# Strassen's seven products in ten of the 32 units of a state-space output projection, and block sums formed in place

## The chip, the core and the metric

The kernel runs on one core of one Trainium2 chip. TensorE (PE) does the matrix multiplications and accumulates in PSUM, which has eight banks of 128 x 512 floats here; ScalarE (ACT) and VectorE (DVE) do the elementwise work; SyncE's queue (SP) issues the weight loads from HBM. The metric is the device time of one execution in microseconds. Of the kernel before, three runs took 1952.21, 1953.63 and 1956.0 us: the median is 1953.63.

## What is computed

One layer of a bidirectional hybrid encoder over 256 tokens with model width 2048: latent attention and a state-space (SSD) branch side by side, gated and mixed, an output projection, then a gated feed-forward with a small convolution, and a final norm. Two places matter here:

```
y = rms_norm(y * silu(z), norm_w)                    # (256, 4096)
s = y @ w_o_ssd                                      # (256, 4096) @ (4096, 2048)
mixed = sigmoid(g_attn) * attn_out + sigmoid(g_ssd) * s
h = h + mixed @ w_out
...
h = h + (silu(gate) * val) @ w_down                  # (256, 5632) @ (5632, 2048)
out = rms_norm(h, norm_final_w)
```

All data are float32. Every product of the dense layers is made of three matrix multiplications on numbers cut into a high part (float32r, the tiles named `...h` or index 0) and the low rest: high x high, high x low and low x high.

## The kernel before

All dense layers are one list of **jobs**; a job owns one weight tile `raw` of up to 1 MB (16 blocks of 128 x 128). A `raw` is loaded by one queue (SP), three of them at a time (`RAWB=3`). It is then cut in **halves** of eight blocks: ScalarE copies a half to `wh` (the high part), VectorE subtracts it from `raw` to give `wl`. Of `wh` and of `wl` there are five buffers each (`HB=5`), so a half can be cut only when TensorE is through with the half five before it. The main loop walks the jobs in order, and before a job's matrix multiplications are issued it asks for the halves up to five ahead (`ahead`, `split_to`). Other work is hung on jobs as side functions (`at(slot, fn)`), and the framework's scheduler settles the final order on each engine; each engine then runs its own list strictly in that order.

**The SSD output projection** (`os`) takes 32 jobs made by `quad`: for each of four groups of 512 output columns, eight jobs of four K tiles. The activations `yHL` are the stationary operand (one 128 x 128 block for 128 tokens), the weights move in blocks of 512 columns; so each job is 4 K tiles x 2 token halves x 3 = 24 matrix multiplications. Each group has two PSUM banks (`g`). When a group ends, `os_evac` scales the sums by the token's norm factor, multiplies by the gate, adds the attention part (`mixS`, reloaded from HBM), and `mix_channels` transposes the result into `mHL`, which the output projection `w_out` then uses. `ssd_split` applies the norm weight and cuts `y` into `yHL` before.

**The down projection** (`w_dn`) already uses Strassen's form (Winograd's variant) in ten jobs, five in each of the first two parts of the feed-forward (`seven_jobs`): a job holds a 256 x 1024 piece of the weights as the four blocks B11, B12, B21, B22, each 128 x 512, and makes seven block products of three matrix multiplications each, 21 in place of 24. The weights' side needs four block sums; `split_seven` forms them in pages of their own, `T13` (B11+B12 and B22+B12) and `T24` (their sum with B22, and that plus B21), in four halves `h` = 0 to 3:

```
if h == 0:   cut B11, B21                      -> products of A11 and A12 use wh/wl
elif h == 1: T1 = B11+B12, T3 = B22+B12; cut T1, T3     (1024 columns)
elif h == 2: T2 = T1+B22, T4 = T2+B21;  cut B22, T2     (512 + 512)
else:        cut T4                                     (512)
```

The activations' sums (`act_sums`) are made when the activations are. In this part of the kernel the seven-product jobs (called S below) alternate with ordinary `w_dn` jobs (called P), whose stationary operand is the weight: 16 matrix multiplications of 512 columns with `wh`, then 16 of 256 columns with `wl`.

Of the kernel before, what the change touches and what calls it, by code (L numbers as in the profile page):

```python
# [47 lines left out]
class Job:  # L48


    def __init__(self, src, nb, mm, evac):
# [12 lines left out]
def tile_bidir_hybrid_layer(ctx: ExitStack, tc, xT, pos, vec, cst, w_in, w_r, w_v, w_qk, w_oa,  # L64
# [53 lines left out]
    def load(i):  # L118
# [26 lines left out]
    sums = {}  # L145

    def split_seven(i, h, wh, wl):
# [32 lines left out]
    def split_to(n):  # L180
        while hptr[0] < min(n, len(halves)):
# [823 lines left out]
    def act_sums(kp, e, o):  # L1005
        t0, t1 = slice(0, P), slice(P, S)
        w = page([P, 4, P], name="asum")
        W1, R, N4, N2 = (w[:, i, :] for i in range(4))
        dve.tensor_sub(W1, e[:, t1], o[:, t1])
        dve.tensor_sub(R, e[:, t1], e[:, t0])  # L1010
        dve.tensor_sub(N2, e[:, t0], W1)
        dve.tensor_sub(N4, o[:, t0], N2)
        t = aS[kp] = page([P, 2, 4, P], F32R, name="aS")
        act.activation(t[:, 0], w, AF.Copy)
# [501 lines left out]
```

## Time and profile before

| | |
|---|---|
| time, median of three runs | 1953.63 us (1952.21 to 1956.0) |
| span of the profiled execution | 1949.9 us |
| PE busy | 1935.2 us, 99% |
| DVE busy | 1502.5 us, 77% |
| ACT busy | 1219.2 us, 63% |

The profile shows one execution. No time of its own is given for that execution beside its span, which is 3.7 us below the median of the timed runs. In rows of the timeline a start and a duration are given in microseconds, then engine, line, operation, tiles and shapes; matrix multiplications are pipelined, so the distance from start to start, not the duration, is what one costs. "[1.12 <-DVE ...]" at a row's end is the idle time of the engine before that instruction and what ended it.

### The profile page before, as it was taken

How to read it: one execution, taken by the hardware profiler on the slowest of the kernel's cores; microseconds unless marked ns; L12 is line 12 of the kernel's file. 1: busy time of each engine (PE TensorE's matmuls, PEld its weight loads, DVE VectorE, ACT ScalarE, POOL GpSimd, SP SyncE). 2: the span in 40 equal slices, each digit the busy share in tenths (PEclk: the TensorE clock that was granted, in tenths of full speed). 3: DMA queues.
4: the chain of work that ended last, by engine and by line, in shares of the span. 5: the costliest groups of instructions: out<-in, count | busy, mean ns of one | idle time of the engine just before them, and what ended most of it. 6: DMA issues, size and time to landing. Idle time of an engine off the chain costs nothing.

```text
span 1949.9 us, 28969 instructions
## 1 busy us (share of the span) xinstructions
PE 1935.2 (99%) x10978; PEld 1695.1 (87%) x10978; DVE 1502.5 (77%) x2498; ACT 1219.2 (63%) x1930; POOL 16.2 (1%) x36
## 2 busy tenths in 40 slices
PE   9999999999999999999999999999999999999997
PEld 8899988888888888888888888888888888888887
DVE  8887765779779879879755566888887887987775
ACT  6566544687887887978644455665555655545563
POOL 0200000000000000000000000000000000000000
PEclk9999999999999999999999999999999999999999
DMA  8644456765665565565666565555556555564553
GB/s 287 200 162 152 136 176 220 248 221 171 213 237 172 198 235 187 202 216 175 207 192 204 197 215 174 194 192 183 185 179 218 186 197 192 181 208 176 204 166 125
DMA packets 103771, 379.57 MB, mean 195 GB/s; under 512 B 11216, under 2 KB 21904, under 8 KB 75472
## 3 DMA queue, kind: packets, MB, share of 16 engines
q1 hardware_dynamic: 101840, 375.09, 56.8%
q8 instruction: 86, 1.41, 0.3%
q0 software_dynamic: 1024, 1.54, 0.3%
q10 hardware_dynamic: 768, 1.09, 0.2%
q14 instruction: 53, 0.43, 0.1%
HBM read 372.08 MB, written 4.42 MB: 193 GB/s over the span
## 4 chain that ended last, share of the span: by engine, by line
PE 96%; DVE 2%; DMA 1%; ACT 1%; issue 0%; SPq 0%; DVEq 0%; ACTq 0%
PE g L224 41%; PE g L231 22%; PE g L259 7%; PE g L260 7%; PE g L261 7%; PE g L203 1%; PE g L205 1%; PE g L204 1%; PE s L853 1%; PE s L862 1%; DMA raw<-in_w_dn 1%; DVE wl L198 1%; PE s L203 0%; PE s L205 0%; PE s L204 0%; PE s L1040 0%
## 5 line engine op out<-in xcount | busy, mean ns | idle before, releaser
L198 DVE TENSOR_TENSOR wl<-raw,wh 128x1024 fp32r<-128x1024 f32 (+2 forms) x654 | 778.9, 1200 | 267.3 <-ACT wh L197 187.5
L197 ACT ACTIVATE wh<-raw 128x1024 fp32r<-128x1024 f32 (+2 forms) x654 | 676.4, 1040 | 375.9 <-PE g L261 156.8
L224 PE MATMUL g<-xHL,wh 128*128 128x512 f32 x1424 | 341.6, 392 | 0.2 <-DVE cu L284 0.2
L224 PE MATMUL g<-hHL,wh 128*128 128x512 f32 x1408 | 327.8, 390 | 0.0
L224 PEld LDWEIGHTS g<-xHL,wh 128*128 128x128 f32 x1424 | 262.5, 188 | 52.0 <-PE s L205 0.4
L224 PEld LDWEIGHTS g<-hHL,wh 128*128 128x128 f32 x1408 | 261.5, 188 | 52.4
L231 PEld LDWEIGHTS g<-xHL,wl 128*128 128x128 f32 x1424 | 182.6, 191 | 7.0
L231 PE MATMUL g<-xHL,wl 128*128 128x256 f32 x1424 | 184.7, 283 | 0.0
L231 PEld LDWEIGHTS g<-hHL,wl 128*128 128x128 f32 x1408 | 174.8, 192 | 3.4
L231 PE MATMUL g<-hHL,wl 128*128 128x256 f32 x1408 | 176.0, 283 | 0.0
L974 DVE SCALAR_TENSOR_TENSOR uc<-u,V,uc 128x255 f32<-128x255 f32 x176 | 84.3, 479 | 57.8 <-ACT uc L972 56.3
L224 PE MATMUL g<-aHL,wh 128*128 128x512 f32 x532 | 127.0, 391 | 1.1 <-DVE aHL L992 1.1
L972 ACT ACTIVATE uc<-u,V 128x256 f32<-128x256 f32 x88 | 52.3, 595 | 115.7 <-DVE u L291 115.7
L224 PEld LDWEIGHTS g<-aHL,wh 128*128 128x128 f32 x532 | 98.4, 188 | 21.7 <-DVE aHL L992 2.3
L259 PE MATMUL g<-wh,xHL 128*128 128x512 f32 x256 | 100.2, 391 | 0.0
L259 PE MATMUL g<-wh,yHL 128*128 128x512 f32 x256 | 100.1, 391 | 0.0
L260 PE MATMUL g<-wl,xHL 128*128 128x512 f32 x256 | 99.9, 390 | 0.0
L261 PE MATMUL g<-wh,yHL 128*128 128x512 f32 x256 | 99.7, 389 | 0.0
L261 PE MATMUL g<-wh,xHL 128*128 128x512 f32 x256 | 99.6, 389 | 0.0
L260 PE MATMUL g<-wl,yHL 128*128 128x512 f32 x256 | 99.6, 389 | 0.0
L231 PEld LDWEIGHTS g<-aHL,wl 128*128 128x128 f32 x532 | 67.9, 191 | 2.4
L231 PE MATMUL g<-aHL,wl 128*128 128x256 f32 x532 | 69.0, 283 | 0.0
(336 smaller groups left out, 2750.2 us busy)
## 6 DMA issues: line engine op xcount, KB each, us to landing
raw<-in_w_in SPq DMA_DIRECT2D x88, 1024.0 KB, 4.9
raw<-in_w_up SPq DMA_DIRECT2D x88, 1024.0 KB, 5.0
raw<-in_w_in SPq DMA_DIRECT2D x128, 256.0 KB, 3.9
raw<-in_w_os SPq DMA_DIRECT2D x128, 256.0 KB, 3.5
raw<-in_w_dn SPq DMA_DIRECT2D x26, 1024.0 KB, 5.1
raw<-in_w_oa SPq DMA_DIRECT2D x64, 256.0 KB, 3.9
FB<-acsD SPq DMA_DIRECT2D x32, 512.0 KB, 7.6
raw<-in_w_out SPq DMA_DIRECT2D x14, 1024.0 KB, 4.9
```

The lines of the kernel that those rows point to most:

```text
L197: act.activation(vh, r, AF.Copy)
L198: dve.tensor_sub(vl, r, f32(vh))
L203: pe.matmul(ps, lhsT=wH, rhs=xH, start=first, stop=False)
L204: pe.matmul(ps, lhsT=wH, rhs=xL, start=False, stop=False)
L205: pe.matmul(ps, lhsT=wL, rhs=xH, start=False, stop=last)
L224: pe.matmul(ps, lhsT=wh[:, b, :], rhs=x, start=k == 0, stop=False)
L231: pe.matmul(cell["ps"][:, 0, :], lhsT=wl[:, b, :], rhs=get(k)[:, 0, :], start=False, stop=k == ktot - 1)
L259: pe.matmul(ps, lhsT=x[:, 0, ts], rhs=wH[:, kk, :], start=k == 0, stop=False)
L260: pe.matmul(ps, lhsT=x[:, 0, ts], rhs=wL[:, kk, :], start=False, stop=False)
L261: pe.matmul(ps, lhsT=x[:, 1, ts], rhs=wH[:, kk, :], start=False, stop=k == kt - 1)
L972: act.activation(o, u, AF.Identity, scale=vcol("fcw", 88 + cb), bias=vcol("fcb", cb))
L974: dve.scalar_tensor_tensor(o[:, a], u[:, b], vcol("fcw", k * 88 + cb), o[:, a], ALU.mult, ALU.add)
```

## The change

- **The projection `os` is rebuilt as two runs** of 16 jobs (`os_run`), run n for output columns 1024n to 1024n+1023. A job holds one pair of K tiles (256 rows) for all eight output blocks. It is either ordinary (24 matrix multiplications) or of seven products (21); both add into the same PSUM banks, four of the pool `g` (M2, M3, M4 and P22) and four of the pool `s` (M1, M5, M6, M7). Four jobs of the first run and six of the second are of seven products; they are written S10, S11, and so on, in the strings `runs`. At the end of a run `inner` and `outer` combine the banks.
- **The block sums of the weights are formed in place** in `raw` by `split_seven`, which the down projection's ten jobs use too; the pages `T13` and `T24` are gone.
- **`ssd_split`** scales `y` in place first (four ScalarE operations of 256 columns) and then cuts it by 512 columns; `ssd_sums` makes the activations' sums for groups 3, 5 and 7 (`ySh`, `ySl`).
- **`os_evac` becomes `mix_in`**, done for a whole run: the first run's two column groups are mixed in the second run, the second run's in the first jobs of `w_out`. For that the first four output blocks of `w_out`, not two, are done in two halves of K, in banks of the pool `s`.
- A job's weights come by one load of 1 MB with pieces of 1 KB, in place of four loads of 256 KB with pieces of 2 KB.

```diff
+    def hilo(wh, wl, v):
+        act.activation(wh, v, AF.Copy)
+        dve.tensor_sub(wl, v, f32(wh))
...
         if h == 0:
-            parts(lambda w: w.rearrange("p (k m) c -> p m k c", k=2), r[:, :4])
+            vh, vl = (w.rearrange("p (k m) c -> p m k c", k=2) for w in (wh, wl))
+            hilo(vh, vl, r[:, :4])
         elif h == 1:
-            t = page([P, 2, 4, P], name="T13")
-            dve.tensor_add(t[:, 0], B11, B12)
-            dve.tensor_add(t[:, 1], B22, B12)
-            parts(both, t)
-            sums["T1"] = t[:, 0]
+            dve.tensor_add(B11, B11, B12)
+            dve.tensor_add(B12, B22, B12)
+            hilo(wh, wl, r[:, :, 0, :])
         elif h == 2:
-            t = page([P, 2, 4, P], name="T24")
-            dve.tensor_add(t[:, 0], sums.pop("T1"), B22)
-            dve.tensor_add(t[:, 1], t[:, 0], B21)
-            parts(one(0), B22)
-            parts(one(1), t[:, 0])
-            sums["T4"] = t[:, 1]
+            dve.tensor_add(B11, B11, B22)
+            hilo(wh[:, :4, :], wl[:, :4, :], B22)
+            hilo(wh[:, 4:, :], wl[:, 4:, :], B11)
         else:
-            parts(one(0), sums.pop("T4"))
+            dve.tensor_add(B21, B11, B21)
+            hilo(wh[:, :4, :], wl[:, :4, :], B21)
...
     def ssd_split(g):
+        y = ypg[g]
+        for k in range(4):
+            act.activation(y[:, k, :], y[:, k, :], AF.Identity, scale=vcol("ssdn", 4 * g + k))
         for b in range(2):
             t = page([P, 2, 2, S], F32R, name="yHL")
-            for j in range(2):
-                k = 2 * b + j
-                w = vcol("ssdn", 4 * g + k)
-                act.activation(t[:, 0, j, :], ypg[g][:, k, :], AF.Identity, scale=w)
-                dve.scalar_tensor_tensor(t[:, 1, j, :], ypg[g][:, k, :], w, f32(t[:, 0, j, :]),
-                                         ALU.mult, ALU.subtract)
+            hilo(t[:, 0], t[:, 1], y[:, 2 * b:2 * b + 2, :])
...
+    SEVEN = ((("M1", "A11"), ("M2", "A12")), (("M5", "W1"), ("M7", "R")), (("M3", "N4"), ("M6", "N2")),
+             (("M4", "A22"),))
...
+        def add(nm, aH, aL, bH, bL):
+            if nm not in M:
+                M[nm] = spsum([P, 512]) if nm in ("M1", "M5", "M6", "M7") else gpsum([P, 512])
+            for x, w in ((aH, bH), (aH, bL), (aL, bH)):
+                pe.matmul(M[nm], lhsT=x, rhs=w, start=left[nm] == total[nm], stop=left[nm] == 1)
+                left[nm] -= 1
+
+        def inner():
+            c, v = page([P, 2, 512], name="m15"), page([P, 2, 512], name="vx")
+            m1, m5, V, X = c[:, 0, :], c[:, 1, :], v[:, 0, :], v[:, 1, :]
+            act.activation(m1, M["M1"], AF.Copy)
+            act.activation(m5, M["M5"], AF.Copy)
+            dve.tensor_sub(V, M["M6"], m1)
+            dve.tensor_add(X, M["M7"], V)
+            dve.tensor_add(V, V, m5)
+            dve.tensor_add(m5, X, m5)
+            res.update({(0, 0): m1, (1, 0): X, (0, 1): V, (1, 1): m5})
+
+        def outer(h):
+            for t, nm in ((0, ("M2", "M3")[h]), (1, ("M4", "P22")[h])):
+                o = res[t, h]
+                dve.tensor_tensor(o, M[nm], o, ALU.subtract if nm == "M4" else ALU.add)
+            cap(n, h, res)
...
-    def os_evac(q, t, ps):
-        if t == 0:
-            mixT[q] = page([P, 2, 512], name="ms")
-        o = mixT[q][:, t, :]
-        act.activation(o, ps, AF.Copy, scale=r_ssd["t"][:, t:t + 1])
-        dve.scalar_tensor_tensor(o, ts_[q][:, t, :], 1.0, o, ALU.add, ALU.mult)
-        dve.tensor_add(o, o, mixS[q][:, t, :])
+    def mix_in(q, res):
+        g = mixT[q] = mixS[q]
+        for t in range(2):
+            o = res[t, q % 2]
+            dve.scalar_tensor_tensor(o, ts_[q][:, t, :], 1.0, o, ALU.add, ALU.mult)
+            dve.scalar_tensor_tensor(g[:, t, :], o, r_ssd["t"][:, t:t + 1], g[:, t, :], ALU.mult, ALU.add)
...
-    at(b + 6, ssd_r)
-    for q in range(4):
-        jobs += quad(lambda m: OsSrc(m), q, 32, lambda k: pair(yHL, k), os_evac)
-        at(len(jobs) + (1 if q < 3 else 2), mix_channels, q)
+    runs = "0 1 2 3 4 5 8 S10 9 S11 6 S14 7 S15 12 13", "0 1 2 3 4 S6 5 S7 8 S10 9 S11 12 S14 S15 13"
...
+    for g, i in ((5, 4), (7, 7), (3, 11)):
+        at(b + i, ssd_sums, g)
...
+    at(b + 17, ssd_r)
+    for q in range(2):
+        at(b + 17 + q, mix_load, q)
+        at(b + 19 + q, lambda q: mix_in(q, done[0]), q)
+        at(b + 20 + q, mix_channels, q)
+        at(b + 25 + q, mix_load, 2 + q)
```

What this makes of the instruction lists is shown at three places on VectorE. The first is the down projection, the third S job of its first part; before, `T13` and `T24` are the pages of block sums, `wl` the low halves of the weights, `h` the residual that an ordinary job adds to:

```order
L166 TENSOR_TENSOR T13_13705<-raw_13671 128x512 [waits DMAHW3_49]
L1099 TENSOR_TENSOR h_11106<-h_11106,g_13632 128x256 [waits PE_49]
L198 TENSOR_TENSOR wl_13674<-raw_13621,wh_13673 128x1024 [waits DMAHW2_49,Activation_49]
L1099 TENSOR_TENSOR h_11106<-h_11106,g_13632 128x256 [waits DVE_49]
L167 TENSOR_TENSOR T13_13705<-raw_13671 128x512
L198 TENSOR_TENSOR wl_13684<-raw_13621,wh_13683 128x1024 [waits Activation_49]
L155 TENSOR_TENSOR wl_13694<-raw_13671,wh_13693 128x4x2x128 [waits Activation_49]
L172 TENSOR_TENSOR T24_13717<-T13_13705,raw_13671 128x512
L155 TENSOR_TENSOR wl_13704<-T13_13705,wh_13703 128x1024 [waits Activation_49]
L173 TENSOR_TENSOR T24_13717<-T24_13717,raw_13671 128x512 [waits DVE_49]
L155 TENSOR_TENSOR wl_13716<-raw_13671,wh_13715 128x512 [waits Activation_49]
L155 TENSOR_TENSOR wl_13716<-T24_13717,wh_13715 128x512 [waits Activation_49]
```

The same S job after the change, where the sums overwrite `raw`:

```order
L148 TENSOR_TENSOR wl_13755<-raw_13732,wh_13754 128x4x2x128 [waits DMAHW5_49,Activation_49]
L159 TENSOR_TENSOR raw_13732<-raw_13732 128x4x128 [waits DVE_49]
L160 TENSOR_TENSOR raw_13732<-raw_13732 128x4x128 [waits DVE_49]
L148 TENSOR_TENSOR wl_13765<-raw_13732,wh_13764 128x1024 [waits Activation_49]
L148 TENSOR_TENSOR wl_13776<-raw_13732,wh_13775 128x512 [waits Activation_49]
L163 TENSOR_TENSOR raw_13732<-raw_13732 128x4x128 [waits DVE_49]
L1159 TENSOR_TENSOR h_11171<-h_11171,g_13782 128x256 [waits PE_49]
L167 TENSOR_TENSOR raw_13732<-raw_13732 128x4x128 [waits DVE_49]
L148 TENSOR_TENSOR wl_13776<-raw_13732,wh_13775 128x512 [waits Activation_49]
L1159 TENSOR_TENSOR h_11171<-h_11171,g_13782 128x256 [waits DVE_49]
L148 TENSOR_TENSOR wl_13808<-raw_13732,wh_13807 128x512 [waits Activation_49]
```

The first two sums no longer stand ahead of the first `wl` with the preceding job's cuts between them; all four stand behind it, and the second `wl` follows the second sum at once.

The second place is VectorE in the new `os` stage, the job S11 of the first run and the ordinary job behind it; before, this stage had only the cuts of ordinary halves (`L198`), two a job:

```order
L148 TENSOR_TENSOR wl_9886<-raw_9851,wh_9885 128x4x2x128 [waits DMAHW4_49,Activation_49]
L159 TENSOR_TENSOR raw_9851<-raw_9851 128x4x128 [waits DVE_49]
L160 TENSOR_TENSOR raw_9851<-raw_9851 128x4x128 [waits DVE_49]
L148 TENSOR_TENSOR wl_9897<-raw_9851,wh_9896 128x1024 [waits Activation_49]
L148 TENSOR_TENSOR wl_9908<-raw_9851,wh_9907 128x512 [waits Activation_49]
L163 TENSOR_TENSOR raw_9851<-raw_9851 128x4x128 [waits DVE_49]
L167 TENSOR_TENSOR raw_9851<-raw_9851 128x4x128 [waits DVE_49]
L148 TENSOR_TENSOR wl_9908<-raw_9851,wh_9907 128x512 [waits Activation_49]
L148 TENSOR_TENSOR wl_9927<-raw_9851,wh_9926 128x512 [waits Activation_49]
L191 TENSOR_TENSOR wl_9946<-raw_9905,wh_9945 128x4x2x128 [waits DMAHW5_49,Activation_49]
L191 TENSOR_TENSOR wl_9956<-raw_9905,wh_9955 128x4x2x128 [waits Activation_49]
```

An S job now has nine VectorE instructions in a row, an ordinary job two.

The third place is VectorE at the end of the second run, behind the job S14: the job S15 (`raw_10749`), the first operation of `inner` (`vx`, from the PSUM bank M6) and the last ordinary job, 13 (`raw_10787`):

```order
L148 TENSOR_TENSOR wl_10790<-raw_10749,wh_10789 128x4x2x128 [waits DMAHW5_49,Activation_49]
L159 TENSOR_TENSOR raw_10749<-raw_10749 128x4x128 [waits DVE_49]
L160 TENSOR_TENSOR raw_10749<-raw_10749 128x4x128 [waits DVE_49]
L148 TENSOR_TENSOR wl_10800<-raw_10749,wh_10799 128x1024 [waits PE_49,Activation_49]
L148 TENSOR_TENSOR wl_10812<-raw_10749,wh_10811 128x512 [waits PE_49,Activation_49]
L163 TENSOR_TENSOR raw_10749<-raw_10749 128x4x128 [waits DVE_49]
L167 TENSOR_TENSOR raw_10749<-raw_10749 128x4x128 [waits DVE_49]
L148 TENSOR_TENSOR wl_10812<-raw_10749,wh_10811 128x512 [waits Activation_49]
L148 TENSOR_TENSOR wl_10825<-raw_10749,wh_10824 128x512 [waits PE_49,Activation_49]
L939 TENSOR_TENSOR vx_10874<-s_10495,m15_10873 128x512 [waits PE_49]
L191 TENSOR_TENSOR wl_10835<-raw_10787,wh_10834 128x4x2x128 [waits DMAHW6_49,Activation_49]
L191 TENSOR_TENSOR wl_10845<-raw_10787,wh_10844 128x4x2x128 [waits Activation_49]
```

Here two S jobs follow one another, and `inner`'s first operation, which waits for TensorE, stands ahead of the cuts of job 13.

## Rows read from the trace of the kernel before

**Rows 1.** The page: busy time by engine (share of the span).

```profile
PE 1935.2 (99%) x10978; PEld 1695.1 (87%) x10978; DVE 1502.5 (77%) x2498; ACT 1219.2 (63%) x1930; POOL 16.2 (1%) x36
```

**Rows 2.** Waits of TensorE: total us, times, longest us.

```profile
PE g L1332 <- DVE xw L335: 1.6, 3, 1.1
PE g L224 <- DVE aHL L992: 1.1, 1, 1.1
...
PE g L224 <- DVE cu L284: 0.2, 1, 0.2
```

**Rows 3.** Windows: length, busy PE, PEld, DVE, ACT, POOL; clock; DMA share, GB/s.

```profile
935.00:1117.00 182.00, 182.00 (x851) 151.41 (x850) 105.29 (x120) 87.83 (x108) 0.00 (x0) 1.00 0.60 194
1400.00:1450.00 50.00, 50.00 (x260) 42.96 (x259) 45.40 (x62) 29.34 (x35) 0.00 (x0) 1.00 0.57 187
1940.00:1949.90 9.90, 0.71 (x4) 0.52 (x4) 5.13 (x10) 0.00 (x0) 0.00 (x0) 0.64 0.55 212
```

**Rows 4.** PE timeline in the old projection, 24 matrix multiplications apart.

```profile
950.00 0.39 PE L259 MATMUL g<-wh,yHL 128*128 128x512 f32 x1
...
955.44 0.39 PE L259 MATMUL g<-wh,yHL 128*128 128x512 f32 x1
```

**Rows 5.** PE timeline in the down projection: S, then P, then S.

```profile
1408.59 0.40 PE L1038 MATMUL s<-wh,aHL 128*128 128x512 f32 x1
...
1413.38 3.79 PE L224 MATMUL g<-aHL,wh 128*128 128x512 f32 x16
1417.01 2.08 PE L231 MATMUL g<-aHL,wl 128*128 128x256 f32 x16
1418.92 0.40 PE L1038 MATMUL s<-wh,aHL 128*128 128x512 f32 x1
```

**Rows 6.** DVE timeline in the down projection, third S job.

```profile
1404.88 0.68 DVE L173 TENSOR_TENSOR T<-T,raw 128x512 f32<-128x512 f32 x1
1405.49 0.68 DVE L155 TENSOR_TENSOR wl<-raw,wh 128x512 fp32r<-128x512 f32 x1
...
1412.68 1.23 DVE L155 TENSOR_TENSOR wl<-raw,wh 128x1024 fp32r<-128x1024 f32 x1
1413.82 0.69 DVE L172 TENSOR_TENSOR T<-T,raw 128x512 f32<-128x512 f32 x1
1414.43 1.22 DVE L155 TENSOR_TENSOR wl<-T,wh 128x1024 fp32r<-128x1024 f32 x1
...
1419.88 0.41 DVE L1099 TENSOR_TENSOR h<-h,g 128x256 f32<-128x256 f32 x1
1420.21 1.22 DVE L198 TENSOR_TENSOR wl<-raw,wh 128x1024 fp32r<-128x1024 f32 x1
```

**Rows 7.** ACT timeline in the same stretch.

```profile
1405.68 0.63 ACT L154 ACTIVATE wh<-T 128x512 fp32r<-128x512 f32 x1 [0.96 <-DVE T L173]
...
1412.95 1.06 ACT L154 ACTIVATE wh<-T 128x1024 fp32r<-128x1024 f32 x1 [0.30 <-PE g L1040]
1413.91 0.62 ACT L154 ACTIVATE wh<-raw 128x512 fp32r<-128x512 f32 x1
```

**Rows 8.** DVE timeline: a single tap, and two taps of which the second needs the first.

```profile
1380.48 1.00 DVE L974 SCALAR_TENSOR_TENSOR uc<-u,V,uc 128x255 f32<-128x255 f32 x2 [1.75 <-ACT uc L972]
...
1387.47 0.47 DVE L974 SCALAR_TENSOR_TENSOR uc<-u,V,uc 128x255 f32<-128x255 f32 x1
1387.87 0.41 DVE L284 TENSOR_TENSOR u<-u,g 128x256 f32<-128x256 f32 x1
```

**Rows 9.** PE timeline: transposes of one `mix_channels`.

```profile
1122.42 1.03 PE L926 MATMUL s<-CT,ms 128*128 128x128 f32 x8
1123.22 2.77 PE L224 MATMUL g<-mHL,wh 128*128 128x512 f32 x10
```

**Rows 10.** PE timeline at the wait for `aHL`.

```profile
1395.01 0.73 PE L224 MATMUL g<-aHL,wh 128*128 128x512 f32 x2 [1.12 <-DVE aHL L992]
```

**Rows 11.** DVE timeline at the same place.

```profile
1393.93 0.69 DVE L166 TENSOR_TENSOR T<-raw 128x512 f32<-128x512 f32 x1 [1.45 <-DMA raw<-in_w_dn]
1394.54 0.42 DVE L992 TENSOR_TENSOR aHL<-uc,aHL 128x256 fp32r<-128x256 f32 x1
```

**Rows 12.** DMA issues: KB each, us from issue to landing.

```profile
raw<-in_w_os SPq DMA_DIRECT2D x128, 256.0 KB, 3.5
raw<-in_w_dn SPq DMA_DIRECT2D x26, 1024.0 KB, 5.1
...
mixS<-mixD SPq DMA_DIRECT2D x4, 512.0 KB, 5.9
```

More of the change, by code (lines that the diff above doesn't have):

```diff
@@ L189, in split_to @@
                 continue
-            if jobs[i].quad:
+            if jobs[i].wide:
+                r = raws[i].rearrange("p (m k) c -> p m k c", m=8)[:, 4 * h:4 * h + 4]
+                vh, vl = (w.rearrange("p (k m) c -> p m k c", k=2) for w in (wh, wl))
+            elif jobs[i].quad:
                 r = raws[i].rearrange("p (m k) c -> p m k c", m=4)[:, :, 2 * h:2 * h + 2, :]
@@ L904, in ssd_split, with sums_of, ssd_sums @@
-            yHL[2 * g + b] = t
+            hilo(t[:, 0], t[:, 1], y[:, 2 * b:2 * b + 2, :])
+            yHL[2 * g + b] = t
+    def sums_of(w, e, o):
+        t0, t1 = slice(0, P), slice(P, S)
+        W1, R, N4, N2 = w
+        dve.tensor_sub(W1, e[..., t1], o[..., t1])
+        dve.tensor_sub(R, e[..., t1], e[..., t0])
+        dve.tensor_sub(N2, e[..., t0], W1)
+        dve.tensor_sub(N4, o[..., t0], N2)
+    yS = {}
+    def ssd_sums(g):
+        y = ypg[g]
+        w = page([P, 4, 2, P], name="ysum")
+        sums_of([w[:, i] for i in range(4)], y[:, 0::2, :], y[:, 1::2, :])
+        hi, lo = page([P, 4, 2, P], F32R, name="ySh"), page([P, 4, 2, P], F32R, name="ySl")
+        hilo(hi, lo, w)
+        for b in range(2):
+            yS[2 * g + b] = hi[:, :, b, :], lo[:, :, b, :]
@@ new lines, in tile_bidir_hybrid_layer, with seven_left, os_run, unit @@
+    SEVEN = ((("M1", "A11"), ("M2", "A12")), (("M5", "W1"), ("M7", "R")), (("M3", "N4"), ("M6", "N2")),
+             (("M4", "A22"),))
+    def seven_left(pr, st, nm):
+        if nm in ("A11", "A12", "A22"):
+            k, t = int(nm[2]) - 1, int(nm[1]) - 1
+            return [pr[:, i, k, t * P:(t + 1) * P] for i in range(2)]
+        i = ("W1", "R", "N4", "N2").index(nm)
+        return [a[:, i, :] for a in st]
+    def os_run(n, order, cap):
+        M, left, res = {}, {}, {}
+        for kp, sv in order:
+            for nm, c in ([(nm, 1) for hh in SEVEN for nm, _ in hh] if sv
+                          else [(nm, 2) for nm in ("M2", "M3", "M4", "P22")]):
+                left[nm] = left.get(nm, 0) + 3 * c
+        total = dict(left)
+        sevens_left = [sum(sv for _, sv in order)]
+        def add(nm, aH, aL, bH, bL):
[19 more added lines that the diff above has]
+            cap(n, h, res)
+        def unit(i, kp, sv):
+            def mm(h, nb, wh, wl):
+                if sv:
+                    for a, (nm, lf) in enumerate(SEVEN[h]):
+                        aH, aL = seven_left(yHL[kp], yS[kp], lf)
+                        add(nm, aH, aL, *(w[:, 4 * a:4 * a + 4, :].rearrange("p m c -> p (m c)")
+                                          for w in (wh, wl)))
+                else:
+                    wH, wL = (w.rearrange("p (k m) c -> p k (m c)", k=2) for w in (wh, wl))
+                    for k in range(2):
+                        for t, nm in ((0, ("M2", "M3")[h]), (1, ("M4", "P22")[h])):
+                            aH, aL = (yHL[kp][:, j, k, t * P:(t + 1) * P] for j in range(2))
+                            add(nm, aH, aL, wH[:, k, :], wL[:, k, :])
+                    if i == len(order) - 1:
+                        outer(h)
+            def ev():
+                if sv:
+                    sevens_left[0] -= 1
+                    if sevens_left[0] == 0:
+                        inner()
+            kh, kk = kp // 8, 2 * kp % 16
+            j = Job(w_os[8 * n:8 * n + 8, kh, :, kk:kk + 2, :].rearrange("m p k c -> p m (k c)"), 16, mm, ev)
+            j.wide, j.seven = True, sv
+            if sv:
+                j.nh = 4
+            return j
+        assert not order[-1][1] and not order[0][1]
+        return [unit(i, kp, sv) for i, (kp, sv) in enumerate(order)]
@@ L1005, in act_sums @@
     def act_sums(kp, e, o):
-        t0, t1 = slice(0, P), slice(P, S)
         w = page([P, 4, P], name="asum")
[L1008 to L1014, printed above, removed]
-        dve.tensor_sub(t[:, 1], w, f32(t[:, 0]))
+        sums_of([w[:, i, :] for i in range(4)], e, o)
+        t = page([P, 2, 4, P], F32R, name="aS")
+        hilo(t[:, 0], t[:, 1], w)
+        aS[kp] = t[:, 0], t[:, 1]
     def seven_jobs(p):
```

63 lines of the change are left out of this document (26 added, 37 removed).

## The prediction

> **What bounds the kernel now.** The page comes first: TensorE is busy 99% of the span, VectorE 77%, ScalarE 63% [rows 1]. The waits of TensorE come next: outside start and end only 1.1 and 0.2 us are lost [rows 2]. So the time is the sum of TensorE's work, and a change gains what it takes off TensorE, minus the waits that it makes. Whether it makes any is read by stage: in the old SSD projection TensorE is busy for 182.00 of 182 us and VectorE for 105.29; in the down projection, where products of seven already run, TensorE is busy for 50.00 of 50 and VectorE for 45.40 [rows 3]. VectorE has room in the first stage and little in the second. An average says nothing about a short chain, so the rest goes by chains. S is a job of seven products, P an ordinary one.
>
> **Off TensorE.** 24 matrix multiplications take 955.44 - 950.00 = 5.44 us, 0.227 each [rows 4]; 21 in an S take 4.79 [rows 5], the same pace. Ten S jobs save 3 each: 30 x 0.227 = 6.8 us. Transposes and the four tiny sums of squares are as many as before.
>
> **Added to VectorE and ScalarE.** On VectorE 1024 columns cost 1.14 us from start to start, 512 cost 0.61 [rows 6]. An S needs two of the first and seven of the second, 6.5 us; a P needs two of the first, 2.3. Ten S: +42 us. The sums of three activation groups (four of 256 columns at 0.33 and one of 1024 each [rows 6]) are +7.4, the two ends of runs +9.7 (16 x 0.61), and cutting y by 512 saves some 3. Together 56 us on 105, in a stage of 182 - 7 = 175: 92%, and waiting within the chains is not yet in it. ScalarE's extra copies fit: 87.83 of 182 was busy [rows 3], and about 25 come on top (1.6 us an S, 1.0 for each of eight groups of y, from the copies' pitch [rows 7]).
>
> **The chain of one S.** Before, the first two sums needed only the load and were done ahead of time; in place they must wait until both engines have read `raw`. From rows: a VectorE operation that needs the one before it starts 0.12 later than a free one (two taps take 1.00, where one takes 0.47 and lets the next start after 0.40) [rows 8]; ScalarE starts 0.12 after the sum that it waits for ended (1404.88 + 0.68 to 1405.68) [rows 6, 7]; its copy of 1024 columns takes 1.06 (0.96 to the next), of 512 0.63 (0.52 to the next) [rows 7]; I let VectorE follow 0.07 later. Counted from the start of the first `wl`:
> - first sum 1.27, second 2.00, ended 2.68; ScalarE copies 2.80 to 3.86; second `wl` 3.93. VectorE stands still for 1.3 us, since the next instruction in its list is this one.
> - `wl` of B22 5.07, third sum 5.68, fourth 6.41, ended 7.09; `wl` of T2 7.17, of T4 7.90.
> - the P behind it: copies from 7.73 and 8.70, `wl` 8.86 and 10.00; the next S at 11.14.
>
> TensorE needs 45 x 0.227 = 10.2 for the pair. So a pair is bound by VectorE and loses 0.9 us, once the cover is used up. **Cover** is the time by which an S's first `wl` is ahead of TensorE's start on that S. The five buffers limit it; before it was 1418.92 - 1412.68 = 6.2 [rows 5, 6]. Needed is: P's first `wl` complete (8.86 + 1.22 = 10.08) when TensorE reaches its 22nd matrix multiplication behind the S's start (5.0): 5.1.
> - **Run 1, pairs S10 to S15:** cover 6.2, 5.3, 4.4: the third waits 0.7, the fourth 0.9: **+1.6** (0.7 to 2.5, as the activation sums of three groups stand in the same stretch).
> - **Run 2, S6 to S11:** 1.03 us of transposes [rows 9] in front of S6 holds TensorE back and restores cover; **+1.0** (0 to 2).
> - **S14 and S15 together, then 13.** S14 has 4.2 of cover left. S15's first `wl` comes at 8.9, its fourth cut at 16.8; then `inner` waits for M6, and the first `wl` of job 13 stands behind that, complete at 19.3. TensorE wants it at 43 x 0.227 = 9.8. Needed 9.5, there 4.2: 5.3; some four products that need only `wh` stand ahead, 0.9: **+4.4** (2.5 to 6).
> - **PSUM and the hand-over to `w_out`:** M5, M7 and M6 need banks that the transposes' cuts free just in time; the second run's mixing has four first halves of `w_out`, some 11 us, as cover: **+0.3** (0 to 1.5). The reload of `mixS` (5.9 us [rows 12]) stands in the same load queue as the weights and may wait for a page, but five ordinary jobs (27 us) cover it.
>
> **The down projection** pays for the sums in place, though the change does not touch its jobs. Its two additions of 256 columns (0.33 each [rows 6]) fill small gaps; the same count gives the next S at 11.35. TensorE takes 10.33 a pair [rows 5]: 1.0 lost. Here P wants `wl` late, and the S's own fourth cut binds: complete at 8.9, wanted at 19 x 0.227 = 4.3, cover needed 4.5. Five S in each of two parts; the first has its gap filled with convolution work. With 6.2 of cover on the second, the last two wait 0.3 and 1.0; with 4.8 the last three 0.7, 1.0 and 1.0. Middle, 2.0, twice: **+4.0** (2.6 to 5.4). One wait goes: TensorE's 1.12 us for `aHL` came from a sum for the second S that waited for its load in front of `aHL` on VectorE [rows 10, 11]; that sum now stands later. **-1.1** (0 to -1.1).
>
> A rule speaks against the 0.12 us: the Trainium skill, page "VectorE: DVE Perf Modes", section "The DRAIN you can't avoid", says a VectorE operation starts only when the one before has drained, and that a semaphore after each costs nothing extra. The trace disagrees: free operations overlap by 0.08 us (1.22 long, 1.14 apart), a dependent one does not [rows 6, 8]. By that rule the three waits inside an S, 0.4 us, would cost nothing; the fourth rival below is that case.
>
> **Sum.** -6.8 + 1.6 + 1.0 + 4.4 + 0.3 + 4.0 - 1.1 = +3.4. Against the profiled execution the span goes from 1949.9 to 1953.3; the timed median is 3.7 higher, and I carry that over: 1953.6 + 3.4 = **1957.0**. With all bounds low the waits are 5.8 less 1.1, and it is 1951.5; with all high 17.4, and it is 1964.2.
>
> **Rivals.**
> - *The cover holds.* VectorE's bare work for two S and the first cut of 13 is 14.2 us, wanted at 9.8, so 6.2 of cover would do if the waits inside the chain were filled by other work. Then only the saving and the lost `aHL` wait are left: 1953.6 - 6.8 - 1.1 = 1945.7; with half of the double S's price (2.2) 1947.9. For it: TensorE never waited among S and P before, at 45.40 of 50 on VectorE [rows 3]. Against: the order shows nothing between second sum and second `wl`.
> - *Clearly slower: the clock.* The granted clock is 1.00 in both busy windows, and 0.64 in the last one, where TensorE did nearly nothing [rows 3]. If the wait at S14, S15, 13 let it fall, those 45 products would take up to twice 0.227, up to 10.2 us more: 1957.0 to 1967. The wait is broken into pieces by products, and 1.1 us of idle [rows 2] left the clock at full; so a small chance. The Trainium skill, page "TensorE: Matmul & The Clock Gate", Part 1, names these two levels and ties the lower one to an idle array; no row here shows a wait this long in mid-kernel.
> - *Clearly slower: loads.* In place, `raw` comes free only with the fourth cut, and its next load is issued then. It lands 5.1 us later [rows 12], and the two jobs between, a P and an S, keep VectorE for some 11 us and cover it. If loads landed late by 0.3 us in each of the 20 S jobs, +6 more: 1963. It decides from 11 us of landing time on, for a single load.
> - *Waits inside VectorE are free.* 0.4 us off each S: run 1, run 2 and both parts lose 0.5, 0.5 and 2.1 in place of 1.6, 1.0 and 4.0, the double S 0.8 less: 1953.
>
> **Chances.** A measurement of this kernel can tell about 0.2% (3.9 us) from no change: faster is below 1949.7, slower above 1957.5. My forecast's case 0.58 (same 0.33, slower 0.25), the cover holds 0.22 (faster 0.20, same 0.02), clock 0.04 and loads 0.08 (slower), free waits 0.08 (same 0.06, faster 0.02). So faster 0.22, same 0.41, slower 0.37. The range reaches from 1947.5, into the first rival, to 1963.5, near my upper bound. The forecast's own range is 1951.5 to 1964.
>
> **What would show it.** In the new profile: 738 products of 512 columns in the projection (768 before), at 0.227; VectorE over 85% there; the waits of TensorE, now on `wl` at the cut helper's subtraction, about 7 us in the projection, most of it behind S14, and about 4 us in the down projection, in the later S of each part; no wait on `aHL`. The distance from an S's first cut to the next S's of about 11.1. If TensorE's waits in the down projection are nil, the chain count is wrong and the time is below 1953; if they are spread over all S jobs alike, loads are at work.

## Result and profile after

The changed kernel takes 1960.74 us (median of seven executions, 1959.09 to 1961.62); the kernel before takes 1953.63 beside it. The ratio is 1.0035, with a 95% interval of 1.0024 to 1.0046: slower by 7.1 us. The profiled span goes from 1949.9 to 1957.3 us. The forecast was 1957.0, so the waits cost 3.7 us more than I counted.

The page of the changed kernel, TensorE's share and the waits of TensorE inside the two stages (engine, line waited for: us in total, times, longest):

```profile
PE 1937.9 (99%) x10948; PEld 1688.1 (86%) x10948; DVE 1562.7 (80%) x2583; ACT 1240.4 (63%) x1975; POOL 16.2 (1%) x36
```

```profile
PE g L1099 <- DVE wl L148: 1.8, 8, 0.3
PE s L931 <- ACT wh L147: 1.5, 2, 1.2
PE g L931 <- DVE wl L191: 1.3, 3, 0.5
...
PE s L931 <- DVE wl L148: 1.0, 3, 0.5
```

Against [rows 2], the wait on `aHL` is gone and waits on `wl` and `wh` have come. These numbers are too small: a matrix multiplication lasts 0.39 us in the record but follows the last one after 0.227, so each wait is about 0.17 us longer than its idle time. What counts is the distance from start to start. From TensorE's timeline I take the start of the first projection product, of the first on `mHL`, of the first on `aHL` and of the closing sums of squares; the table gives the distances. It holds all kernels of this study, each profiled once (the last column is the ratio to the kernel before, with its interval).

| kernel | projection | to `aHL` | down projection and rest | ratio |
|---|---|---|---|---|
| before | 181.66 | 268.89 | 551.75 | 1 |
| after | 181.67 | 270.02 | 557.92 | 1.0035 (1.0024 to 1.0046) |
| e1: pages in the down projection | 182.44 | 270.28 | 550.97 | 0.9997 (0.9988 to 1.0006) |
| e2: before, sums in place | 181.66 | 268.90 | 558.63 | 1.0028 (1.0018 to 1.0038) |
| e3: pages everywhere | 174.78 | 270.28 | 551.02 | 0.9964 (0.9951 to 0.9976) |
| e4: no double S | 178.84 | 271.53 | 558.00 | 1.0023 (1.0014 to 1.0032) |
| e6: six buffers | 184.64 | 271.74 | 551.37 | 1.0033 (1.0020 to 1.0045) |
| e7: one S in each run | 179.40 | 271.97 | 558.19 | 1.0030 (1.0019 to 1.0041) |
| e8: half cuts | 175.17 | 271.05 | 550.69 | 0.9968 (0.9957 to 0.9980) |
| e9: half cuts, no double S | 174.84 | 269.70 | 550.67 | 0.9963 (0.9950 to 0.9977) |

So after the change **the projection takes as long as before**: the 6.8 us saved, and the 0.8 us of one `mix_channels` that now lies behind it (from start to start in [rows 9]; its bar of 1.03 overlaps the next), are all eaten by waits. **The down projection, which the change left as it was but for the sums, loses 6.2 us net.**

The windows of [rows 3] in the changed kernel (same columns; first the projection, then the down projection):

```profile
935.00:1117.00 182.00, 177.96 (x814) 143.72 (x812) 154.97 (x197) 99.03 (x126) 0.00 (x0) 1.00 0.60 186
1400.00:1450.00 50.00, 48.74 (x236) 38.96 (x235) 43.99 (x60) 27.92 (x35) 0.00 (x0) 1.00 0.52 176
```

VectorE is at 85% in the projection, and in the down projection it is *less* busy than before (43.99, not 45.40), while TensorE waits for it: VectorE stands still itself. The clock is 1.00 in both.

The down projection's rows that answer to [rows 5], TensorE's timeline at the start of an S, the product that waits for the low half of its third sum, and the next two S:

```profile
1408.68 0.40 PE L1098 MATMUL s<-wh,aHL 128*128 128x512 f32 x1
1412.76 0.50 PE L1099 MATMUL g<-wl,aS 128*128 128x512 f32 x1 [0.26 <-DVE wl L148]
...
1419.98 0.40 PE L1098 MATMUL s<-wh,aHL 128*128 128x512 f32 x1
...
1431.24 0.40 PE L1098 MATMUL s<-wh,aHL 128*128 128x512 f32 x1
```

A pair of S and P takes 11.30 and 11.26 us, where it took 10.33. VectorE at the same S (answers to [rows 6]), and one row of ScalarE (to [rows 7]):

```profile
1404.86 1.22 DVE L148 TENSOR_TENSOR wl<-raw,wh 128x1024 fp32r<-128x1024 f32 x1
1406.11 0.69 DVE L159 TENSOR_TENSOR raw<-raw 128x512 f32<-128x512 f32 x1
1406.84 0.69 DVE L160 TENSOR_TENSOR raw<-raw 128x512 f32<-128x512 f32 x1
1408.74 1.83 DVE L148 TENSOR_TENSOR wl<-raw,wh 128x1024 fp32r<-128x1024 f32 x2 [1.21 <-ACT wh L147]
1410.48 0.69 DVE L163 TENSOR_TENSOR raw<-raw 128x512 f32<-128x512 f32 x1
...
1416.11 1.22 DVE L148 TENSOR_TENSOR wl<-raw,wh 128x1024 fp32r<-128x1024 f32 x1
```

```profile
1407.65 1.58 ACT L147 ACTIVATE wh<-raw 128x1024 fp32r<-128x1024 f32 x2 [3.20 <-DVE raw L160]
```

This is the chain that the prediction counted: second sum at +1.98 (counted 2.00), second `wl` at +3.88 (3.93), the next S at +11.25 (11.35). In between VectorE idles for 1.21 us: ScalarE can copy only when the second sum is done, and VectorE has only the cut of that copy next in its list.

### The profile page after: what moved, and what is told of

Read it like the earlier page. It is cut to its first block, busy times and chain, and to the rows that moved or that the text cites. A ratio compares the mean times of both kernels' runs of the same rounds, so it can differ in the third digit from the quotient of the medians.

```text
span 1957.3 us, 28870 instructions
## 1 busy us (share of the span) xinstructions
PE 1937.9 (99%) x10948; PEld 1688.1 (86%) x10948; DVE 1562.7 (80%) x2583; ACT 1240.4 (63%) x1975; POOL 16.2 (1%) x36
## 3 DMA queue, kind: packets, MB, share of 16 engines
q0 software_dynamic: 1024, 1.54, 0.3%
q10 hardware_dynamic: 768, 1.09, 0.2%
## 4 chain that ended last, share of the span: by engine, by line
PE 90%; DVE 6%; ACT 2%; DMA 1%; issue 1%; SPq 0%; ACTq 0%; DVEq 0%
PE g L217 39%; PE g L224 20%; PE g L931 6%; PE g L252 4%; PE g L253 4%; PE g L254 4%; DVE wl L191 2%; DVE wl L148 1%; PE s L931 1%; PE g L196 1%; PE g L198 1%; PE g L197 1%; ACT wh L190 1%; PE s L836 1%; PE s L845 1%
## 5 line engine op out<-in xcount | busy, mean ns | idle before, releaser
L191 DVE TENSOR_TENSOR wl<-raw,wh 128x1024 fp32r<-128x1024 f32 (+1 forms) x634 | 753.2, 1202 | 202.2 <-ACT wh L190 127.5
L190 ACT ACTIVATE wh<-raw 128x1024 fp32r<-128x1024 f32 (+1 forms) x634 | 651.4, 1038 | 276.4 <-PE g L217 102.2
L147 ACT ACTIVATE wh<-raw 128x512 fp32r<-128x512 f32 (+1 forms) x100 | 78.2, 798 | 101.5 <-DVE raw L160 53.5
L931 PE MATMUL g<-wh,yHL 128*128 128x512 f32 x392 | 125.6, 391 | 0.3 <-DVE m L948 0.3
L148 DVE TENSOR_TENSOR wl<-raw,wh 128x512 fp32r<-128x512 f32 (+1 forms) x100 | 88.5, 902 | 26.5 <-ACT wh L147 22.0
L931 PEld LDWEIGHTS g<-wh,yHL 128*128 128x128 f32 x392 | 73.5, 188 | 16.0 <-issue 0.7
L931 PE MATMUL g<-wl,yHL 128*128 128x512 f32 x196 | 76.9, 393 | 1.3 <-DVE wl L191 1.3
```

The source lines that it names most:

```text
L147: act.activation(wh, v, AF.Copy)
L148: dve.tensor_sub(wl, v, f32(wh))
L190: act.activation(vh, r, AF.Copy)
L191: dve.tensor_sub(vl, r, f32(vh))
L931: pe.matmul(M[nm], lhsT=x, rhs=w, start=left[nm] == total[nm], stop=left[nm] == 1)
```

## Experiments

**Theory.** The waits come from the hand-over inside an S: with the sums in place, VectorE makes two sums, ScalarE copies 1024 columns, VectorE cuts them, one behind the other. **Rivals:** VectorE's bare work is too much; `raw` is held longer and loads come late; in the down projection, something that the rebuilt `os` moved there.

**e1 and e2: whose waits are those in the down projection?** e1 is the changed kernel with pages in these ten jobs (`paged` set in `seven_jobs`), e2 the kernel before with `split_seven` alone replaced by the new one.

```diff
+        elif jobs[i].paged and h == 1:
+            t = page([P, 2, 4, P], name="T13")
+            dve.tensor_add(t[:, 0], B11, B12)
+            dve.tensor_add(t[:, 1], B22, B12)
...
+            hilo(vh, vl, t)
+            sums["T1"] = t[:, 0]
```

> The changed kernel, with the block sums of the down projection's ten jobs of seven products (S) written to pages of their own again (T13, T24), as in the kernel before; the projection os keeps its sums in place. Theory (in place, the second wl stands right behind the two sums that ScalarE's copy needs, and VectorE idles through the hand-over): the S starts in the down projection are 10.33 us apart again, not 11.25, and the last mm3 product comes 6.3 to 7.4 us earlier (7.4 of waits gone, the 1.1 us wait for aHL perhaps back): 1953.4 to 1954.5. Rival (the down projection waits because raw is released late and loads land late, or for something that the rebuilt os moved into it): no change, 1960.7.

> The kernel before, with split_seven alone taken from the changed kernel: block sums in place, no pages T13 and T24; the projection os is the old one. Theory: only the down projection differs; the S starts 11.25 us apart for the last four of each part, +7.4, the wait for aHL gone, -1.1: 1959.9 (1.0032). Rival (the rebuilt os causes the down projection's waits): 1953.6 (1.000).

e1 took 1953.16 us (expected 1953.4 to 1954.5), e2 1958.53 (1959.9). The stage shrinks from 557.92 to 550.97 us in e1 and grows from 551.75 to 558.63 in e2, with the old `os`. So the in-place sums alone make the loss in this stage. The wait for `aHL`, which I had thought to be either back or gone, is 0.3 us in e1's waits; in e2, where I expected none, it is 0.6 us, in the second part. e2's 5.5 us in the timed runs is 1.4 less than its stage shows, within its interval. e1's projection is 0.8 us longer than the changed kernel's, at the hand-over between the two runs of `os` (1.1 us in its waits). e1 has as many VectorE operations as the changed kernel (2583 on both pages), and its window of the down projection has TensorE busy throughout, as before the change:

```profile
1400.00:1450.00 50.00, 50.00 (x258) 42.87 (x258) 45.50 (x63) 29.50 (x35) 0.00 (x0) 1.00 0.57 188
```

**e3: pages in the projection too.** The condition `paged` is dropped. VectorE's operations stay the same in number and size, only their operands and their order change.

> The changed kernel with the block sums of all S jobs, of os too, written to pages of their own (T13, T24), ahead of the first wl where the load is there. Theory (the hand-over to ScalarE and back makes the waits, not VectorE's bare work): beside the 7.5 us that pages in the down projection gave back, run 1's 1.6 and run 2's 0.9 go, and the 4.5 around S14, S15, 13 shrink to 0 to 1.5: 1953.2 - 2.5 - 3.0 to 4.5 = 1946.2 to 1947.7. Rival (VectorE's bare work, the same in number and size, is too much for os): the os stage stays at 181.4 us and the time at 1953.2. Second rival (the pages are short, so that cuts or mixS wait for one): over 1953.

It took 1946.38 us, the low end of what the theory gave. The projection's window:

```profile
935.00:1117.00 182.00, 181.68 (x855) 150.93 (x853) 159.68 (x208) 103.94 (x130) 0.00 (x0) 1.00 0.64 195
```

The stage takes 174.78 us, 6.9 less, and the only wait of TensorE among its products is 0.32 us (0.6 from start to start); behind S14 there is none. VectorE has *more* to do in this window than after the change (159.68, not 154.97), since more of the program fits in. Its bare work was not the bound.

**e4: the two S in a row undone.**

```diff
-"0 1 2 3 4 S6 5 S7 8 S10 9 S11 12 S14 S15 13"
+"0 1 2 3 4 S6 5 S7 8 S10 9 S11 12 14 S15 13"
```

> The changed kernel, with unit 14 of the second run as an ordinary job, so that no two S jobs follow one another (nine S in place of ten). Theory (two S in a row use up the cover): TensorE gets 3 products more, +0.7; from the start of 14 to the end of 13 waits fall from 4.5 to about 0.9 (what a single S after S11 lost in the first run): 1960.7 + 0.7 - 3.6 = 1957.8. Rival (the waits there come from inner's hand-over behind the last S, whatever stands ahead of it): 1960.5 to 1961.4.

It took 1957.86 us. From the start of 14 to the end of 13, 69 products (15.66) take 15.75 us: nearly all of the 4.5 us of waits is gone, more than the 3.6 that I expected. The stage shrinks by 2.83 us only, since three products (0.7) came on top and 0.9 is given back at the hand-over between the runs; 1.2 more is given back at the mixing in `w_out`. So the whole time came out as expected with parts that did not (TensorE's timeline; the same hand-over had 0.29 after the change):

```profile
1026.49 0.47 PE L931 MATMUL g<-wh,yHL 128*128 128x512 f32 x1 [1.23 <-DVE m L948]
...
1121.35 0.98 PE L1000 MATMUL g<-CT,mixS 128*128 128x128 f32 x7 [1.21 <-DVE mixS L992]
```

**e6: more cover.** Six buffers for `wh` and `wl`; one page and two small tiles pay for it, so the edit is not a pure one.

```diff
-RAWB=3, HB=5, NPG=29, NP1=18
+RAWB=3, HB=6, NPG=28, NP1=16
```

> The changed kernel with six in place of five buffers for wh and for wl, paid for with one page of 4 KB (28, not 29) and two small tiles. Theory (a pair of S and P runs at VectorE's chain, 11.25 us, but loses time only when the cover is used up): the chain per pair stays, each run of S starts with 1.4 to 2.7 us more cover, so the waits shrink by about that in each part of the down projection and at each stretch of os: 3.7 to about 1.7 a part, 1.6 and 0.9 to 0 in os, 4.5 to about 2.3 at the double S: 1960.7 - 4.0 - 2.5 - 2.2 = 1952, less what the missing page costs in earlier stages (0 to 3). Rival (each S loses 0.93 whatever the cover, from its second cut or from loads): 1960.7 or more.

It took 1960.41 us, where the theory gave 1952 and the rival 1960.7. The number is the rival's, but the stages say otherwise: the sum hides opposite things. The trace is of the slowest of its five executions (1962.18). In the down projection the loss is gone altogether (551.37), more than I expected. VectorE's chain is as slow as before, but TensorE does not feel it; VectorE's first cuts of three S, then TensorE's first products of the same:

```profile
1410.80 1.22 DVE L148 TENSOR_TENSOR wl<-raw,wh 128x1024 fp32r<-128x1024 f32 x1
...
1421.95 1.22 DVE L148 TENSOR_TENSOR wl<-raw,wh 128x1024 fp32r<-128x1024 f32 x1
...
1433.04 1.22 DVE L148 TENSOR_TENSOR wl<-raw,wh 128x1024 fp32r<-128x1024 f32 x1
```

```profile
1417.95 0.40 PE L1098 MATMUL s<-wh,aHL 128*128 128x512 f32 x1
...
1428.27 0.40 PE L1098 MATMUL s<-wh,aHL 128*128 128x512 f32 x1
...
1438.60 0.40 PE L1098 MATMUL s<-wh,aHL 128*128 128x512 f32 x1
```

VectorE takes 11.15 and 11.09 us a pair, TensorE 10.32 and 10.33; the distance between cut and use is 7.15, then 6.32, then 5.56. That is the cover, seen being used up at 0.8 us a pair, and the last S comes before it falls under the 4.5 that is needed (4.64 there). In the projection the single waits of both runs are gone too, as expected; at the double S 3.9 us are left, where I expected 2.3. Elsewhere e6 loses: the projection begins 4.6 us later (939.89, after the change 935.33), and in it TensorE stands still for 3.7 us at the hand-over between the runs:

```profile
1032.75 0.77 PE L931 MATMUL g<-wh,yHL 128*128 128x512 f32 x1 [3.68 <-DVE m L948]
1033.31 0.63 PE L931 MATMUL g<-wl,yHL 128*128 128x512 f32 x1
1033.74 1.06 PE L931 MATMUL g<-wh,yHL 128*128 128x512 f32 x2
1034.59 0.63 PE L931 MATMUL g<-wl,yHL 128*128 128x512 f32 x1
```

The wait costs more than its length. The products behind it follow one another after 0.427 us, not 0.227 (three in 1.28 from 1033.31 to 1034.59), and the granted clock there, in the window from 1032.75 to 1038.50, is 0.50 (columns as in [rows 3]):

```profile
1032.75:1038.50 5.75, 5.75 (x14) 4.55 (x15) 5.75 (x10) 0.00 (x0) 0.00 (x0) 0.50 0.69 209
```

The 24 products of that job take 8.31 us, where the next job takes 5.44: 2.9 us more. The same happens once far ahead of the projection, and makes about 4 of its 4.6 us of delay: TensorE waits for `vl` (L628), and the products behind that wait run at the lower clock too (0.50 from 111 to 113 us):

```profile
110.24 0.80 PE L252 MATMUL g<-wh,xHL 128*128 128x512 f32 x1 [2.16 <-DVE vl L628]
```

In no other trace here does the clock fall, start and end apart. What makes `vl` late, the sixth buffer or the page and small tiles that pay for it, stays open.

At the hand-over VectorE's rows show why: `inner`'s first operation (L939), which stands ahead of `outer`'s (L948) in the list, starts at 1030.60 here and at 1017.45 after the change. Five more cuts stand in front of it, and VectorE idles 2.27, 1.56 and 0.57 us for ScalarE's copies among them.

**e7: what do eight of the ten S bring?** Only S10 is left in each run.

```diff
-"0 1 2 3 4 5 8 S10 9 S11 6 S14 7 S15 12 13", "0 1 2 3 4 S6 5 S7 8 S10 9 S11 12 S14 S15 13"
+"0 1 2 3 4 5 8 S10 9 11 6 14 7 15 12 13", "0 1 2 3 4 6 5 7 8 S10 9 11 12 14 15 13"
```

> The changed kernel with one S in each run of os (S10 in both) in place of four and six, the other eight as ordinary jobs; sums in place as in the changed kernel. Theory (the eight S save 8 x 0.68 = 5.4 us of products and cost 7.0 of waits within os): os takes 181.4 + 5.4 - 7.0 = 179.8 us, and the time goes from 1960.7 to about 1959; VectorE in os falls below 80%. Rival (the saving is bigger than the waits): 1962 or more. Second rival (waits at the ends of the runs stay or grow, since the combining stands where it stood): 1961 to 1964.

It took 1959.19 us, as expected, and VectorE is busy for 126.68 of the 182 us (70%). The stage is 2.27 us *shorter* with eight S fewer: they save 5.4 us of products and cost 7.7 of waits. Most of this comes back as one wait of 2.08 us behind the stage. It follows a cut that ScalarE starts at 1128.35 only, after 5.64 us of idle time; why that cut is late I did not take apart:

```profile
1131.32 1.42 PE L217 MATMUL s<-mHL,wh 128*128 128x512 f32 x5 [2.08 <-DVE mHL L1003]
```

So in whole times e7 and the changed kernel cannot be told apart (1.0030 and 1.0035), and the stage's own distances carry the reading.

**e8 and e9: the hand-over alone.** Sums stay in place in all jobs; the second cut goes in two halves, so that ScalarE copies the first sum while VectorE makes the second. On each engine one operation of 1024 columns becomes two of 512, which is a little more work. e9 also has unit 14 as an ordinary job.

```diff
             dve.tensor_add(B11, B11, B12)
+            act.activation(wh[:, :4, :], B11, AF.Copy)
             dve.tensor_add(B12, B22, B12)
-            hilo(wh, wl, r[:, :, 0, :])
+            act.activation(wh[:, 4:, :], B12, AF.Copy)
+            dve.tensor_sub(wl[:, :4, :], B11, f32(wh[:, :4, :]))
+            dve.tensor_sub(wl[:, 4:, :], B12, f32(wh[:, 4:, :]))
```

> The changed kernel, sums in place in all S jobs, with the second cut of an S in two halves: ScalarE copies the first sum's 512 columns while VectorE makes the second sum, and VectorE subtracts in two halves of 512. Theory (VectorE idles 1.2 us an S for ScalarE's copy of 1024 columns that can start only behind the second sum): VectorE's distance from S to S in the down projection falls from 11.25 to 10.2 to 10.4, about TensorE's 10.33; waits there fall from 7.4 to 0 to 1, in os run 1 and 2 from 2.5 to under 0.5, at the double S from 4.5 by about 2: 1960.7 - 6.9 - 2.2 - 2.0 = 1949.6, though no work is taken away (on both engines 0.07 us an S is added). Rival (VectorE's bare work is the bound): no change or a little slower, 1960.7 to 1962. Second rival (in place as such: raw held late, loads late): 1960.7.

> Half cuts as in the run beside it, and unit 14 of the second run as an ordinary job. Theory: the products of one more ordinary job cost 0.7, the rest of the waits behind S14 (about 2.0 with half cuts) goes, some 1.2 come back at the mixing in w_out, as they did when the double S was undone alone: 1949.6 + 0.7 - 2.0 + 0.5 to 1.2 = 1949 to 1949.5. Faster than the kernel before (1953.0) by 0.2%. Rival (double S costs nothing any more with half cuts): 1950.3 or more against 1949.6.

e8 took 1947.06 us, some 13 less than the changed kernel and faster than the kernel before. VectorE in the down projection, one S from its first cut to the second half of its second cut (L164), and the start of the next S; then ScalarE in the same S:

```profile
1410.02 1.22 DVE L148 TENSOR_TENSOR wl<-raw,wh 128x1024 fp32r<-128x1024 f32 x1
1411.27 0.69 DVE L159 TENSOR_TENSOR raw<-raw 128x512 f32<-128x512 f32 x1
1411.99 0.69 DVE L161 TENSOR_TENSOR raw<-raw 128x512 f32<-128x512 f32 x1
1412.74 0.69 DVE L163 TENSOR_TENSOR wl<-raw,wh 128x512 fp32r<-128x512 f32 x1
1413.35 0.69 DVE L148 TENSOR_TENSOR wl<-raw,wh 128x512 fp32r<-128x512 f32 x1
1413.95 0.69 DVE L164 TENSOR_TENSOR wl<-raw,wh 128x512 fp32r<-128x512 f32 x1
...
1420.18 1.22 DVE L148 TENSOR_TENSOR wl<-raw,wh 128x1024 fp32r<-128x1024 f32 x1
```

```profile
1412.07 0.63 ACT L160 ACTIVATE wh<-raw 128x512 fp32r<-128x512 f32 x1 [2.48 <-DVE raw L159]
1412.61 0.62 ACT L147 ACTIVATE wh<-raw 128x512 fp32r<-128x512 f32 x1
1413.13 0.62 ACT L162 ACTIVATE wh<-raw 128x512 fp32r<-128x512 f32 x1
```

No idle time is left in front of these cuts (in the window 1400 to 1450 VectorE idled for 4.8 us before the cuts of S after the change, in the projection for 12.4; here for none and 3.4), and a pair takes VectorE 10.16 us (1410.02 to 1420.18; expected 10.2 to 10.4), less than TensorE's 10.33. No idle time of TensorE for `wl` or `wh` is listed any more in either stage. I had expected some 2 us to stay at the double S; from start to start 0.7 stays (66 products, 15.0 us, in 15.64), which is part of why e8 beat 1949.6. This also ends the rival of late loads: `raw` is held to the fourth cut as in the changed kernel, and TensorE waits for none of it.

The windows of [rows 3] in e8 show a VectorE that is busier than in any other kernel here, and no TensorE that waits for it:

```profile
935.00:1117.00 182.00, 181.84 (x848) 149.94 (x847) 161.53 (x214) 103.50 (x139) 0.00 (x0) 1.00 0.63 195
1400.00:1450.00 50.00, 50.00 (x260) 42.98 (x259) 48.88 (x70) 28.34 (x39) 0.00 (x0) 1.00 0.61 200
```

e9 took 1945.86 us (1945.50 to 1946.68; e8 1946.61 to 1948.25), the fastest median here: 0.9963 of the kernel before (0.9950 to 0.9977), and 3.1 us below the 1949 expected. 2.5 of that is e8's own. By the stages its gain over e8 lies in `w_out` (269.70 against 271.05), where I had expected a loss: e8 waits 0.22 us there for `mixS` and 0.39 for `mHL`, 1.1 us from start to start, and e9 for neither. In the projection e9 has three products (0.7) more and is still 0.3 shorter, so the double S cost e8 about 1.0, half of what I had expected; the rival, that it costs nothing, fell. In whole times the two are not clearly apart: their intervals overlap.

## Why the prediction was right or wrong

Forecast 1957.0, measured 1960.74; inside the range and inside the forecast's own range, but on the side to which I gave 0.37 (slower), not the 0.41 of no change. The mechanism was the one forecast; one term of the sum was too small. Step by step:

- **The saving, -6.8:** right. With waits gone the projection takes 174.78 (e3) and 175.17 (e8); 181.66 less 6.8 and less the 0.8 of the moved `mix_channels` is 174.1, and small waits (0.6 in e3, 1.0 in e8) make the rest.
- **Run 1, +1.6:** two holes of TensorE, on the third and fourth pair, as the prediction had them, but smaller. The third pair takes 10.78 us from start to start, where it takes 10.20 without waits (e3, e8), the fourth 11.01: 0.6 and 0.8, **1.4**.
- **Run 2, +1.0:** one hole of 0.8 behind S11, and 0.1 before it: 0.9.
- **S14, S15, 13, +4.4:** from the start of S14 to the end of 13 some 19.5 us pass for 66 products (15.0): 4.5. All of these in TensorE's timeline:

```profile
1003.16 0.50 PE L931 MATMUL g<-wl,yHL 128*128 128x512 f32 x1 [0.29 <-DVE wl L191]
1014.18 0.50 PE L931 MATMUL g<-wl,yHL 128*128 128x512 f32 x1 [0.48 <-DVE wl L191]
1025.41 0.47 PE L931 MATMUL g<-wh,yHL 128*128 128x512 f32 x1 [0.29 <-DVE m L948]
1092.13 0.50 PE L931 MATMUL g<-wl,yHL 128*128 128x512 f32 x1 [0.50 <-DVE wl L191]
1103.17 0.50 PE L931 MATMUL s<-wl,yHL 128*128 128x512 f32 x1 [0.51 <-DVE wl L148]
1105.77 0.74 PE L931 MATMUL s<-wh,ySh 128*128 128x512 f32 x2 [1.18 <-ACT wh L147]
```

- **PSUM and hand-over, +0.3:** the third row above, 0.45 from start to start, and 0.2 at `mHL`: 0.6. e4, e6 and e7 show that this place is touchy: 1.2, 3.7 and 2.1 us, once the order around it shifts, and in e6 the clock on top.
- **The down projection, +4.0: the term that failed.** It measured 7.4, 3.7 a part, outside the 2.6 to 5.4 that I gave it. The mechanism and the chain were right; the cover was not. I took 4.8 to 6.2 us on the second S and needed 4.5. It was 3.8: first `wl` at 1404.86, TensorE at 1408.68. The count then gives 0.7, 1.0, 1.0 and 1.0 for the last four S, 3.7; measured are 1.0, 0.9, 0.9 and 0.9, the same sum. (TensorE stops twice in each: for the third sum's low half, as in the row at 1412.76, and for the fourth cut, which alone I had counted.) What I left out stands one S earlier, in VectorE's timeline:

```profile
1394.37 0.42 DVE L1066 TENSOR_TENSOR aHL<-uc,aHL 128x256 fp32r<-128x256 f32 x1 [0.63 <-ACT aHL L1065]
1396.58 1.23 DVE L148 TENSOR_TENSOR wl<-raw,wh 128x1024 fp32r<-128x1024 f32 x1 [1.78 <-PE g L224]
```

  The first S's second cut had to wait until TensorE came to the low products of the two ordinary jobs in front, as I read it for a buffer. Before, VectorE made the first two sums of the next S here, before that S was cut ([rows 11] has one of them), and the second S had 6.0 us of cover (TensorE at 1408.59 [rows 5]):

```profile
1402.61 1.22 DVE L155 TENSOR_TENSOR wl<-raw,wh 128x1024 fp32r<-128x1024 f32 x1
```

  In place those sums come later. So the part starts with less cover, not with that of the third S before the change, which I had carried over from [rows 5, 6].
- **aHL, -1.1:** right; there is no such wait in the changed kernel.

The measured terms, -6.8 + 1.4 + 0.9 + 4.5 + 0.6 + 7.4 - 1.1, make +6.9, where +3.4 was forecast. The medians differ by 7.1, the spans by 7.4.

The rivals: **the cover holds** fell, but the times that it gave (1945.7 to 1947.9) are close to those of e3, e8 and e9 (1945.86 to 1947.06), in which TensorE hardly waits. **The clock** stayed at 1.00 in both windows through all waits of the changed kernel, the longest of which was 1.18 us. But what this rival feared does happen: in e6, behind 3.68 us of idle time, the products took 0.427 in place of 0.227, about the "twice" of the prediction. **Loads** fell with e8. **Waits inside VectorE are free** fell too: in the changed kernel the sum that waits for the one before it starts 0.73 us after it (1406.11, 1406.84), where free operations of this size start 0.60 to 0.61 apart (1412.74, 1413.35, 1413.95 in e8), once more 0.12. The Trainium skill's page "VectorE: DVE Perf Modes", section "The DRAIN you can't avoid", says of eight copies in a row that a semaphore after each costs nothing extra; here an operation that waits for the one before it does pay. The same section adds that a following operation that is not held starts earlier, which I had not weighed in the prediction, and with that the overlap of the free operations agrees. But this was never the big part: three such waits are 0.4 us an S, the idle time behind ScalarE's copy is 1.21.

## What to carry to other kernels

Making a sum in place saves a page but can put a producer, a copy on another engine and its consumer directly behind one another in one engine's list; look there for the idle time of the *feeding* engine, and cut the step in halves before taking work away. A feeder that is slower than TensorE for a while costs nothing until its lead is used up, so read the lead at the first job of the stretch, with the edit's own new waits in it, and count from there. And a saving of products in a stage that feeds from one engine is worth only what that feeder's chain, not its busy share, lets through.

## What was not expected of the hardware

- Two operations of 512 columns in place of one of 1024, on both engines, made VectorE's chain per pair 1.09 us shorter (11.25 to 10.16) though each engine had a little more to do; in twenty S jobs it gave some 13 us (by the ratios, 1.0035 and 0.9968).
- VectorE at 161.53 of 182 us (89%) and 48.88 of 50 (98%) left TensorE without a listed wait on its cuts (e8); at 43.99 of 50 TensorE waited in every pair.
- One buffer more moved a combining operation from 1017.45 to 1030.60 on VectorE, and TensorE's wait for a bank from 0.3 to 3.7 us. Behind that wait the granted clock was 0.50, and one job's 24 products took 8.31 us in place of 5.44.
